# High-weight and low-weight products of a half of K issued in two runs of eight instead of in alternation

## The chip, the cores and the metric

The kernel runs on one core of one Trainium2 chip. The metric is the device time of one execution in microseconds (us); lower is better. Engine names in profile rows: PE is TensorE's products, PEld its weight loads, DVE is VectorE, ACT is ScalarE, POOL is GpSimd, SP is SyncE.

## The reference

A decoder trunk of two layers over 256 tokens of width 2048, in float32. Layer 0 has causal self-attention with 16 heads of 128, a T5 relative bias (with 256 tokens there is one block, so no gathered blocks); layer 1 has sliding-window attention (window 128) with 4 shared K/V heads and a sink for each head. Each layer then has a ConvFFN, and a LayerNorm follows each of the four parts:

```python
attn = moba_attention(h, ...) if layer < N_A_LAYERS else swa_attention(h, ...)
h = layer_norm(ALPHA * h + attn, ln_g[layer, 0], ln_b[layer, 0])
u = h @ w_up                               # 2048 -> 2 * 5504
hc = causal_depthwise_conv3(u) + conv_b
g, v = jnp.split(hc, 2, axis=-1)
h = layer_norm(ALPHA * h + (gelu(g) * v) @ w_down, ln_g[layer, 1], ln_b[layer, 1])
```

Nearly all of the arithmetic is `x @ W` with 256 rows of x and some 95 million weights, each of which is read once.

## The kernel before

**Precision.** Every float32 operand of a large product is split into a high part, its rounding to fp32r, and a low part, the rest. A product x @ W is made of three: high x with high W, low x with high W, high x with low W. `xT` holds x transposed, [128, 16 blocks of K, 512]: columns 0 to 255 are the high parts of the 256 tokens, columns 256 to 511 the low parts.

**Weights.** They arrive as one stream of halves, each [128, 1024] float32 (512 KB). SyncE loads a half into one of 4 `raw` buffers (L71), ScalarE copies it to the high part `wh` (L85), VectorE subtracts to get the low part `wl` (L86); there are 4 buffers of each. `take` hands out the next half, after it has issued the splits up to 3 halves ahead.

**Two kinds of unit.** Where the output is wanted transposed (Q and K in attention, the up-projection of the FFN) the weights are stationary: `ws_unit` makes 128 output features for 256 tokens from two halves, each eight blocks of K by 128 features. For each block j a 128x128 block of `wh` is loaded and 512 columns of `xT` stream through it (high and low x, into columns 0 to 511 of the accumulator `acc`, L224), and then the same block of `wl` is loaded and the 256 high columns stream (added to columns 0 to 255, L225). There are 222 such units, 444 halves: 32 units in attention of layer 0, 85 in each FFN and 20 in attention of layer 1. The first unit of each FFN goes another way (the `feed` branch, L203 to L219): all of its products have 256 columns, first alternating high and low weights (L208, L209), then sixteen with the high weights and the low x (L213). V and the output projections use activations as the stationary side (`Moving`): three products of 512 columns for each block (L244, L245, L246).

**Order.** The schedule is written out by hand: each engine runs its instructions in program order. `step` marks a slot at the end of each half; `at` puts work of ScalarE and VectorE into a later slot (it is issued by the next `take`, behind the splits), `pe_at` puts TensorE work of attention there. After a unit ScalarE copies columns 256 to 511 of `acc` (L532), VectorE adds columns 0 to 255 (L533), and in the FFN the convolution, gelu and gate follow (L534 to L543).

Of the kernel before, what the change touches and what calls it, by code (L numbers as in the profile page):

```python
# [46 lines left out]
def trunk(ctx: ExitStack, tc: tile.TileContext, wst, xT_in, x_in, relb, onehot, umask, sinks, conv_in, ln_g, ln_b, out):  # L47
# [26 lines left out]
    def split_upto(i):  # L74
        while todo["split"] <= min(i, n_halves - 1):
            s = todo["split"]
            r = raws.pop(s)
            if s in aside:
                j = aside.pop(s)
                wh, wl = (xT[:, k:k + 2, :].rearrange("p a b -> p (a b)") for k in (4 * j, 4 * j + 2))  # L80
            else:
                wh = spool.tile([P, HW], F32R, name="wh")
                wl = spool.tile([P, HW], F32R, name="wl")
            for c in pieces(s):
                nc.scalar.activation(wh[:, c], r[:, c], AF.Copy)  # L85
                nc.vector.tensor_tensor(out=wl[:, c], in0=r[:, c], in1=wh[:, c].bitcast(F32), op=ALU.subtract)  # L86
            halves[s] = (wh, wl)
            todo["split"] += 1
            load_weights()
# [13 lines left out]
    def run(agenda):  # L103
        for n in sorted(n for n in agenda if n <= slot["now"]):
            for f, a in agenda.pop(n):
                f(*a)

    def step():
        run(behind)
        slot["now"] += 1  # L110
# [3 lines left out]
    def take(ahead=AHEAD):  # L114
        i = nexth["i"]
        nexth["i"] += 1
        split_upto(i + ahead)
        run(before)
        return halves.pop(i)
# [75 lines left out]
    def ws_unit(acc, feed=None):  # L195

        def cols(w, j):
            return w[:, j * P:(j + 1) * P]  # L200

        o = acc[:, 0:T]
        if feed:  # L203
            pair = [take(1 - i) for i in range(2)]
            for k in range(KB):
                feed(k)
                wh, wl = pair[k // 8]
                nc.tensor.matmul(o, cols(wh, k % 8), xT[:, k, 0:T], start=(k == 0), stop=False)  # L208
                nc.tensor.matmul(o, cols(wl, k % 8), xT[:, k, 0:T], start=False, stop=False)  # L209
            feed(KB)  # L210
            split_upto(nexth["i"] + AHEAD - 2)
            for k in range(KB):
                nc.tensor.matmul(o, cols(pair[k // 8][0], k % 8), xT[:, k, T:2 * T], start=False, stop=(k == KB - 1))  # L213
                if k % 8 == 7:
                    step()
                    split_upto(nexth["i"] + AHEAD - 2 + (k + 1) // 8)
                    if k < 8:
                        run(before)
            return  # L219
        for hf in range(2):  # L220
            wh, wl = take()
            for j in range(8):
                k = hf * 8 + j
                nc.tensor.matmul(acc, cols(wh, j), xT[:, k, :], start=(k == 0), stop=False)  # L224
                nc.tensor.matmul(o, cols(wl, j), xT[:, k, 0:T], start=False, stop=(k == KB - 1))  # L225
            step()

# [208 lines left out]
    def layer_attention(l, rest):  # L436
        with tc.tile_pool(name=f"att{l}", bufs=2) as pool:
# [24 lines left out]
            def feat_unit(name, bufs):  # L462
                acc = acc_tile()
                ws_unit(acc)
                o = pool.tile([P, T], F32, name=name, bufs=bufs)

                def evac():
                    nc.scalar.activation(o, acc[:, T:2 * T], AF.Copy)
                    nc.vector.tensor_tensor(out=o, in0=acc[:, 0:T], in1=o, op=ALU.add)

                at(0, evac, first=True)
                return o
# [35 lines left out]
    def layer_ffn(l, rest):  # L508
        with tc.tile_pool(name=f"ffn{l}", bufs=2) as pool:
# [35 lines left out]
            for i in range(FT):  # L545
                g, v = (pool.tile([P, T], F32, name=f"c{s}") for s in range(2))
                for s, c in enumerate((g, v)):
                    first = i == 0 and s == 0
                    acc = acc_tile()
                    ws_unit(acc, feed if first else None)  # L550
                    at(0, conv, i, s, acc, first, c)
                    if s == 0:
                        at(1, nc.scalar.activation, c, c, AF.Gelu_apprx_tanh)
                at(0, gate, i, g, v)
                at(1, store, i, g)
# [93 lines left out]
```

## Time and profile before

| | |
|---|---|
| time, median of 3 runs | 2125.76 us (2123.73 to 2126.88) |
| profiled execution | 2124.89 us, span 2123.0 us |
| busy, share of the span | TensorE products 99%, weight loads 84%, VectorE 68%, ScalarE 47%, GpSimd 1% |
| HBM read | 401.02 MB, 192 GB/s over the span |

The span goes from the first to the last instruction. A weight load and the products around it overlap, and a product is recorded as busy for longer than the time until the next one starts; so two busy TensorE lines together exceed the span.

### The profile page before, as it was taken

To read this page: it belongs to the slowest core of one execution; us is meant where nothing else is said; L and a number is where in the kernel's file an instruction comes from. 1 tells how busy PE (TensorE), PEld (TensorE's weight loads), DVE (VectorE), ACT (ScalarE), POOL (GpSimd) and SP (SyncE) were. 2 spreads that over 40 slices of the span, in tenths; PEclk is the share of its full clock that TensorE was granted. 3 is DMA by queue.
4 is the path that set the end of the run, shared out by engine and by line. 5 is a ranking of instruction groups with operands and counts; after the bars stand their busy time and mean duration, and the time that the engine had idled before them with its cause. 6 is when DMAs were issued, how large, how long until landed. Compare 5 with 4: busy or idle time off the path is not lost.

```text
span 2123.0 us, 28513 instructions
## 1 busy us (share of the span) xinstructions
PE 2092.1 (99%) x10962; PEld 1785.8 (84%) x10962; DVE 1434.8 (68%) x2104; ACT 987.6 (47%) x1395; POOL 25.5 (1%) x40
## 2 busy tenths in 40 slices
PE   8999999999999999999999999999999999999997
PEld 6888888788888888888887888888888888888886
DVE  5555555787777787744456676687787787765455
ACT  5444444354445544433344554445544454443342
POOL 1100000000000000000001000000000000000000
PEclk9999999999999999999999999999999999999999
DMA  8855556565555555556666644565555555556663
GB/s 278 300 170 177 169 169 204 178 200 188 187 188 187 184 186 188 188 188 197 192 206 211 212 145 162 174 211 187 184 187 187 189 184 183 188 190 196 191 196 130
DMA packets 114120, 405.08 MB, mean 191 GB/s; under 512 B 15504, under 2 KB 15808, under 8 KB 112704
## 3 DMA queue, kind: packets, MB, share of 16 engines
q1 hardware_dynamic: 106848, 383.83, 55.6%
q0 software_dynamic: 7136, 19.44, 2.6%
q8 instruction: 86, 1.41, 0.3%
q14 instruction: 50, 0.41, 0.1%
HBM read 401.02 MB, written 6.34 MB: 192 GB/s over the span
## 4 chain that ended last, share of the span: by engine, by line
PE 97%; DVE 2%; ACT 0%; DMA 0%; issue 0%; SPq 0%; ACTq 0%; DVEq 0%
PE acc L224 39%; PE acc L225 20%; PE acc L245 11%; PE acc L246 11%; PE acc L244 11%; PE at L386 1%; PE at L419 1%; DVE wl L86 1%; PE at L412 0%; PE at L385 0%; DMA raw<-in_wst_dram 0%; PE at L420 0%; DVE xT L332 0%; DVE res L316 0%; DVE res L315 0%; PE at L325 0%
## 5 line engine op out<-in xcount | busy, mean ns | idle before, releaser
L86 DVE TENSOR_TENSOR wl<-raw,wh 128x1024 fp32r<-128x1024 f32 (+1 forms) x709 | 865.4, 1222 | 609.9 <-ACT wh L85 609.4
L224 PE MATMUL acc<-xT,wh 128*128 128x512 f32 x3552 | 1262.9, 401 | 0.0
L85 ACT ACTIVATE wh<-raw 128x1024 fp32r<-128x1024 f32 (+1 forms) x709 | 750.6, 1059 | 936.2 <-PE acc L246 331.7
L225 PE MATMUL acc<-xT,wl 128*128 128x256 f32 x3552 | 997.5, 281 | 0.0
L224 PEld LDWEIGHTS acc<-xT,wh 128*128 128x128 f32 x3552 | 667.8, 188 | 163.7
L225 PEld LDWEIGHTS acc<-xT,wl 128*128 128x128 f32 x3552 | 671.7, 189 | 0.9
L244 PE MATMUL acc<-wh,aT 128*128 128x512 f32 x656 | 255.7, 390 | 0.0
L246 PE MATMUL acc<-wh,aT 128*128 128x512 f32 x656 | 255.4, 389 | 0.0
L245 PE MATMUL acc<-wl,aT 128*128 128x512 f32 x656 | 255.4, 389 | 0.0
L246 PEld LDWEIGHTS acc<-wh,aT 128*128 128x128 f32 x656 | 123.1, 188 | 25.6
L244 PEld LDWEIGHTS acc<-wh,aT 128*128 128x128 f32 x656 | 123.2, 188 | 25.5
L245 PEld LDWEIGHTS acc<-wl,aT 128*128 128x128 f32 x656 | 123.2, 188 | 25.4
L244 PE MATMUL acc<-wh,oT 128*128 128x512 f32 x224 | 89.0, 398 | 0.0
L246 PE MATMUL acc<-wh,oT 128*128 128x512 f32 x224 | 87.4, 390 | 0.0
L245 PE MATMUL acc<-wl,oT 128*128 128x512 f32 x224 | 87.3, 390 | 0.0
L535 DVE SCALAR_TENSOR_TENSOR c<-h,cw,c 128x255 f32<-128x255 f32 x170 | 82.3, 484 | 6.0
L536 DVE SCALAR_TENSOR_TENSOR c<-h,cw,c 128x254 f32<-128x254 f32 x170 | 82.2, 484 | 6.1
L534 DVE TENSOR_SCALAR c<-h,cw 128x256 f32<-128x256 f32 x170 | 70.2, 413 | 6.1
L244 PE MATMUL acc<-wh,xT 128*128 128x512 f32 x160 | 65.9, 412 | 8.3 <-ACT wh L85 8.1
L533 DVE TENSOR_TENSOR h<-acc,h 128x256 f32<-128x256 f32 x170 | 71.0, 418 | 0.0
L542 ACT ACTIVATE aT<-c 128x256 fp32r<-128x256 f32 x86 | 36.0, 419 | 66.3 <-DVE c L539 66.3
L245 PE MATMUL acc<-wl,xT 128*128 128x512 f32 x160 | 64.1, 400 | 1.5 <-DVE wl L86 1.5
(102 smaller groups left out, 1193.3 us busy)
## 6 DMA issues: line engine op xcount, KB each, us to landing
raw<-in_wst_dram SPq DMA_DIRECT2D x723, 512.0 KB, 3.4
band<-ud POOLq DMA_DIRECT2D x8, 512.0 KB, 13.2
bias<-band POOLq DMA_DIRECT2D x8, 512.0 KB, 5.0
gb<-in_ln_g_dram POOLq DMA_DIRECT2D x4, 1024.0 KB, 5.8
gb<-in_ln_b_dram POOLq DMA_DIRECT2D x4, 1024.0 KB, 8.6
res<-in_x_dram POOLq DMA_DIRECT2D x2, 1024.0 KB, 9.6
out_dram<-res SPq DMA_DIRECT2D x8, 256.0 KB, 2.5
xc<-in_xT_dram SPq DMA_DIRECT2D x7, 256.0 KB, 7.3
```

The source lines that it names most:

```text
L85: nc.scalar.activation(wh[:, c], r[:, c], AF.Copy)
L86: nc.vector.tensor_tensor(out=wl[:, c], in0=r[:, c], in1=wh[:, c].bitcast(F32), op=ALU.subtract)
L224: nc.tensor.matmul(acc, cols(wh, j), xT[:, k, :], start=(k == 0), stop=False)
L225: nc.tensor.matmul(o, cols(wl, j), xT[:, k, 0:T], start=False, stop=(k == KB - 1))
L244: nc.tensor.matmul(acc, sh, wh, start=(k == 0), stop=False)
L245: nc.tensor.matmul(acc, sh, wl, start=False, stop=False)
L246: nc.tensor.matmul(acc, sl, wh, start=False, stop=(k == self.nk - 1))
L533: nc.vector.tensor_tensor(out=h, in0=acc[:, 0:T], in1=h, op=ALU.add)
L534: nc.vector.tensor_scalar(c, h, w[:, 2:3], w[:, 3:4], op0=ALU.mult, op1=ALU.add)
L535: nc.vector.scalar_tensor_tensor(c[:, 1:T], h[:, 0:T - 1], w[:, 1:2], c[:, 1:T], op0=ALU.mult, op1=ALU.add)
L536: nc.vector.scalar_tensor_tensor(c[:, 2:T], h[:, 0:T - 2], w[:, 0:1], c[:, 2:T], op0=ALU.mult, op1=ALU.add)
L542: nc.scalar.activation(aT[:, i, 0:T], g, AF.Copy)
```

## The change

In `ws_unit` the loop over the eight blocks of a half is split in two: first the eight products with `wh`, then the eight with `wl`. Operands, accumulator and the number of instructions are the same; `start` is still on the first product of the unit and `stop` on the last. The `feed` branch and `Moving` stay.

```diff
             for j in range(8):
                 k = hf * 8 + j
                 nc.tensor.matmul(acc, cols(wh, j), xT[:, k, :], start=(k == 0), stop=False)
+            for j in range(8):
+                k = hf * 8 + j
                 nc.tensor.matmul(o, cols(wl, j), xT[:, k, 0:T], start=False, stop=(k == KB - 1))
             step()
```

## Rows read from the trace of the kernel before

**Rows 1.** The page, parts 1 (busy us, share, instructions) and 4 (chain, shares).
```profile
PE 2092.1 (99%) x10962; PEld 1785.8 (84%) x10962; DVE 1434.8 (68%) x2104; ACT 987.6 (47%) x1395; POOL 25.5 (1%) x40
...
PE 97%; DVE 2%; ACT 0%; DMA 0%; issue 0%; SPq 0%; ACTq 0%; DVEq 0%
PE acc L224 39%; PE acc L225 20%; PE acc L245 11%; PE acc L246 11%; PE acc L244 11%; PE at L386 1%; PE at L419 1%; DVE wl L86 1%; PE at L412 0%; PE at L385 0%; DMA raw<-in_wst_dram 0%; PE at L420 0%; DVE xT L332 0%; DVE res L316 0%; DVE res L315 0%; PE at L325 0%
```

**Rows 2.** The page, costliest groups: count | busy us, mean ns | idle before.
```profile
L224 PE MATMUL acc<-xT,wh 128*128 128x512 f32 x3552 | 1262.9, 401 | 0.0
...
L225 PE MATMUL acc<-xT,wl 128*128 128x256 f32 x3552 | 997.5, 281 | 0.0
L224 PEld LDWEIGHTS acc<-xT,wh 128*128 128x128 f32 x3552 | 667.8, 188 | 163.7
L225 PEld LDWEIGHTS acc<-xT,wl 128*128 128x128 f32 x3552 | 671.7, 189 | 0.9
```

**Rows 3.** Line L224 in two stretches: count, durations, first and last start (us).
```profile
L224 PE MATMUL acc<-xT,wh x1303: 394/398/404, 419.6 to 879.7; 128*128 128x512 f32 x187
...
L224 PE MATMUL acc<-xT,wh x1331: 394/398/404, 1399.8 to 1869.7; 128*128 128x512 f32 x191
```

**Rows 4.** Timeline of TensorE, FFN of layer 0: start us, duration us, instruction.
```profile
816.06 0.40 PE L224 MATMUL acc<-xT,wh 128*128 128x512 f32 x1
816.29 0.28 PE L225 MATMUL acc<-xT,wl 128*128 128x256 f32 x1
816.41 0.40 PE L224 MATMUL acc<-xT,wh 128*128 128x512 f32 x1
816.65 0.28 PE L225 MATMUL acc<-xT,wl 128*128 128x256 f32 x1
816.77 0.40 PE L224 MATMUL acc<-xT,wh 128*128 128x512 f32 x1
817.01 0.28 PE L225 MATMUL acc<-xT,wl 128*128 128x256 f32 x1
817.12 0.40 PE L224 MATMUL acc<-xT,wh 128*128 128x512 f32 x1
```

**Rows 5.** Timeline of TensorE, attention of layer 0: first and ninth L224.
```profile
63.12 0.39 PE L224 MATMUL acc<-xT,wh 128*128 128x512 f32 x1
...
65.89 0.39 PE L224 MATMUL acc<-xT,wh 128*128 128x512 f32 x1
```

**Rows 6.** Timeline, down-projection of layer 0: first and fifteenth L244.
```profile
1000.07 0.39 PE L244 MATMUL acc<-wh,aT 128*128 128x512 f32 x1
...
1009.59 0.39 PE L244 MATMUL acc<-wh,aT 128*128 128x512 f32 x1
```

**Rows 7.** First unit of layer 1's FFN: loads of L213, and the timeline.
```profile
L213 PEld LDWEIGHTS acc<-xT,wh x16: 192/192/193, 1394.2 to 1396.0; 128*128 128x128 f32 x16
...
1394.32 2.08 PE L213 MATMUL acc<-xT,wh 128*128 128x256 f32 x16
1396.24 0.40 PE L224 MATMUL acc<-xT,wh 128*128 128x512 f32 x1
1396.47 0.28 PE L225 MATMUL acc<-xT,wl 128*128 128x256 f32 x1
```

**Rows 8.** Timeline: first and ninth of two streams of 512-column products.
```profile
888.49 0.40 PE L244 MATMUL acc<-wh,aT 128*128 128x512 f32 x1
...
890.36 0.40 PE L246 MATMUL acc<-wh,aT 128*128 128x512 f32 x1
...
86.25 0.39 PE L245 MATMUL acc<-wl,xT 128*128 128x512 f32 x1
...
88.10 0.39 PE L244 MATMUL acc<-wh,xT 128*128 128x512 f32 x1
```

**Rows 9.** Busy by stretch (granted clock, DMA, GB/s last); waits, 420 to 880 us.
```profile
408.00:888.00 480.00, 480.00 (x2719) 416.36 (x2718) 379.33 (x595) 238.05 (x340) 0.00 (x0) 1.00 0.59 191
...
ACT wh L85 <- PE acc L224: 63.3, 77, 1.1
```

## The prediction

> **What bounds the kernel now.** I read the page first. TensorE is busy for 2092.1 of 2123.0 us, and the chain that ended last is 97% TensorE: 39% lies on the high-weight product L224, 20% on the low-weight product L225 [rows 1]. So a gain or loss shows in the time only if it changes how fast one product follows the other on TensorE. A busy share of 99% does not say that the engine is at its best: the products overlap, so the number to read is the distance from one start to the next, not the duration. The list of costly groups gives durations of 401 and 281 ns for products that stream 512 and 256 columns, each with a weight load of its own of 188 or 189 ns, 3552 of each kind [rows 2].
>
> Next I took the distance between starts. In the up-projection of both FFNs, where nothing but these pairs runs on TensorE, 1303 starts of L224 span 419.6 to 879.7 us: 460.1 / 1302 = 0.3534 us a pair; the second layer gives 469.9 / 1330 = 0.3533 us [rows 3]. Half a unit (eight pairs) takes 8 x 0.3534 = 2.827 us. The timeline shows how a pair divides: the 512-column product holds the engine for 0.23, 0.24, 0.24 us in turn, the 256-column one for 0.12, 0.12, 0.11 us, and the pattern comes back after three pairs (816.06 to 817.12 us = 1.06 us) [rows 4].
>
> Then I looked for what either product costs among its own kind. A settled stream of 512-column products (the down-projection) runs 14 triples from 1000.07 to 1009.59 us: 9.52 / 42 = 0.2267 us each [rows 6]. Sixteen 256-column products in a row, L213, which read the same xT with a new weight block each, take 1394.32 to 1396.24 us: 1.92 / 16 = 0.120 us each, although their loads are recorded at 192 ns, so the loads overlap what goes before [rows 7]. The two add up to 0.3467 us, 6.7 ns below the pair of today. Alternating need not cost that much more: in one half in attention eight pairs run from 63.12 to 65.89 us, 0.346 us each [rows 5]. So TensorE has two ways through the same instructions, and the FFNs are in the slower one. That is not the clock: the granted clock is 1.00 over the FFN up-projection [rows 9].
>
> **What the change does, part by part.** It removes nothing and adds nothing: the same 7104 products with the same loads, in another order. Per half there are now eight 512-column products, then eight 256-column ones, so sixteen changes of width become two.
>
> *The eight low-weight products.* 8 x 0.120 = 0.960 us by L213 [rows 7]. The last of them is followed by a 512-column product; the alternation shows 0.11 to 0.12 us there [rows 4], so this end is right within 0.01 us.
>
> *The eight high-weight products.* If they ran settled from the first one on: 8 x 0.2267 = 1.813 us. But the trace shows that a 512-column stream does not settle at once. Behind the pairs of the FFN, the first eight of the down-projection run from 888.49 to 890.36 us: 1.87 us, 0.057 above settled. Behind the small products of attention (after the first one, which also waits them out), eight run from 86.25 to 88.10 us: 1.85 us, 0.037 above [rows 8]. Eight products in a row are thus mostly inside this settling. Which entry fits? No row has a run of 512s behind a run of 256s; the nearest is the one L224 behind the sixteen L213, and it held the engine for 0.23 us (1396.24 to 1396.47 us) [rows 7], not 0.24 as the first one at 888.49 us. So I take 1.85 us and keep 1.813 and 1.87 us as ends.
>
> *Half a unit after:* 1.85 + 0.96 = 2.81 us against 2.827: a gain of 0.017 us. Ends: 1.813 + 0.96 = 2.773 (gain 0.054) and 1.87 + 0.96 = 2.83 (loss 0.003).
>
> *How often.* 85 units x 2 halves x 2 FFN layers = 340 halves; at 0.017 us: 5.8 us. The other 52 units (104 halves) lie in attention, where some halves run at 0.346 us a pair already [rows 5] and would lose 2.81 - 2.77 = 0.04 us, and others run as the FFN's do. I take one in four as fast (a choice): 104 x (0.75 x 0.017 - 0.25 x 0.04) = 0.3 us. Together 6.1 us.
>
> *Waits.* No wait is added. The wait for the low weights moves from the second product of a half to the ninth, which only relaxes it. The high-weight buffer is read for the last time by the eighth product instead of the fifteenth: from 7 x 0.353 = 2.47 us into the half to 7 x 0.23 = 1.6 us, about 0.9 us earlier. ScalarE waits for just that in 77 cases between 420 and 880 us, 63.3 us in total [rows 9], so its next copy (L85) starts earlier, with the evacuation of the previous unit queued behind it. I cost this at nothing: ScalarE is busy 238.05 of 480 us and VectorE 379.33 of 480 there, while TensorE is busy for all 480 [rows 9], so copies already lead the products. The low-weight buffer is still freed by the last product of the half and the raw buffer after VectorE's split, so the loads start no earlier and collide with nothing new; 191 GB/s becomes some 1% more at most [rows 9]. If that cover were gone, the cost would show as TensorE idle before L224 or L225, and both stand at 0.0 us now [rows 2].
>
> [...] The rows give the product N/2.4 GHz plus 13 ns, for 512 columns (213 + 13) and for 256 (107 + 13) [rows 6, 7]. [...]
>
> **Sum.** Profiled execution before: 2124.89 us, with 2123.0 us of span and 1.9 us around it; the median of the runs is 2125.76, 0.9 us more, which I leave as scatter. 2124.9 - 6.1 = 2118.8 us.
>
> **Rivals.**
> 1. *Runs settle at once.* The slow way needs the alternation, and an eight runs at 0.2267 us each. For it: settled streams and L213 hold their pace over a whole run [rows 6, 7]. Against: the two settlings of rows 8. Time: 340 x 0.054 = 18.4 us, plus at most 78 x 0.054 = 4.2 us in attention: 2124.9 - 22.6 = 2102.3 us.
> 2. *The settling eats it all, or order is neutral.* At 1.87 us a run, the entry seen behind the FFN's pairs [rows 8], halves lose 0.003 us: +1 us, and the fast halves of attention (26 x 0.06) another 1.6 us: 2127.5 us; strictly neutral: 2124.9. For it: 1.87 is the entry behind the very same weights and data layout. Against: the first product behind L213 takes 0.23, not 0.24 us [rows 7]. [...]
> 3. *Slower: every high-weight product keeps its slow gap.* Place: L224. Today's 0.23, 0.24, 0.24 us (mean 0.2367) would belong to a 512-column product in this stage, and the 0.11 to 0.12 of the 256s, which give part of it back, would become a flat 0.120. Then a half takes 8 x (0.2367 + 0.120) = 2.853 us, +0.026: 340 x 0.026 = 8.8 us, and in attention up to 104 x 0.026 = 2.7: 2136.4 us. It decides once eight 512s take over 2.827 - 0.96 = 1.867 us, 0.2334 each. For it: L224 is recorded with 0.40 us in the FFN against 0.39 for the settled stream [rows 4, 6], and the first one behind L213 is already slow [rows 7]. Against: fast pairs exist with the same operands [rows 5], and the settling of rows 8 falls with every product.
>
> **How the numbers follow.** Chances: partial settling, my forecast, 45% (own range 2111 to 2121 us, an entry cost of 0.015 to 0.045 us a half); rival 1, 15%; rival 2, 25%; rival 3, 15%. The predicted time is the first: 2118.8 us. The range reaches down to rival 1, 2103, and up past rival 2 into the lower part of rival 3, 2130 us; outside stay most of rival 3 and the last of rival 1, together under 2 in 10. A change of under 0.2% (4.25 us) can't be told from none here. Faster than that: nearly all of the first case (its top edge lies at the bound, 2120.6) and rival 1: 57%. Within 0.2%: rival 2 and that edge: 27%. Slower: rival 3 and a tail of rival 2: 16%.
>
> **What would show it.** In the profile after, starts of the high-weight products in an FFN: my forecast wants the eight of a half to take about 1.85 us, with gaps near 0.235 first and near 0.228 last, and the eight low-weight ones 0.96. Gaps of 0.227 from the first on are rival 1; 1.87 us is rival 2; a steady 0.237 is rival 3. TensorE's idle before the two lines should stay near 0, and the down-projections, the norms and the granted clock as they are. I am wrong if the eight low-weight products don't hold 0.120 us behind 512-column ones, of which no row speaks, or if a wait for weights appears before TensorE.

## The result and the profile after

The median is 2110.04 us (4 runs, 2109.25 to 2110.67) against 2124.82 us before (4 runs beside them): a ratio of 0.9929, 95% interval 0.9912 to 0.9946. The kernel became 0.7% faster: 14.8 us where 6.1 were forecast. The time lies inside the range (2103 to 2130), in the first case's direction and just below its own range (2111 to 2121).

The page after, parts 1 and 4, and of part 5 the lines that answer to [rows 2] (L224 is still the high-weight product, L227 is now the low-weight one; the lines behind it moved down by two):

```profile
PE 2077.3 (99%) x10962; PEld 1788.2 (85%) x10962; DVE 1434.7 (68%) x2104; ACT 989.1 (47%) x1395; POOL 25.5 (1%) x40
...
PE 97%; DVE 2%; ACT 0%; issue 0%; DMA 0%; SPq 0%; ACTq 0%; DVEq 0%
...
L224 PE MATMUL acc<-xT,wh 128*128 128x512 f32 x3552 | 896.3, 394 | 0.0
L224 PEld LDWEIGHTS acc<-xT,wh 128*128 128x128 f32 x3552 | 640.8, 189 | 116.0
L227 PEld LDWEIGHTS acc<-xT,wl 128*128 128x128 f32 x3552 | 484.5, 190 | 34.8
L227 PE MATMUL acc<-xT,wl 128*128 128x256 f32 x3552 | 495.2, 282 | 0.0
```

The same 10962 products, still 97% of the chain, and no idle time of TensorE before either line; the mean high-weight product is recorded with 394 ns instead of 401. Do not read a gain out of the busy column: 1262.9 became 896.3 us only because neighbours of one line now overlap and are counted once. The distance between starts is again the number to read. Timeline of TensorE after, in the FFN of layer 0; the second and third lines come from narrow windows (from 421.93 and from 422.16 us) and show the fifth and the sixth of the eight products:

```profile
420.82 2.00 PE L224 MATMUL acc<-xT,wh 128*128 128x512 f32 x8
421.75 0.39 PE L224 MATMUL acc<-xT,wh 128*128 128x512 f32 x1
421.98 0.39 PE L224 MATMUL acc<-xT,wh 128*128 128x512 f32 x1
422.66 1.12 PE L227 MATMUL acc<-xT,wl 128*128 128x256 f32 x8
423.61 0.63 PE L224 MATMUL acc<-xT,wh 128*128 128x512 f32 x2
```

Eight high-weight products take 422.66 - 420.82 = 1.84 us: the first four 0.93 us (0.2325 each), the last four 0.91 (0.2275), so the settling of [rows 8] is there. It is over after five products: the last three take 422.66 - 421.98 = 0.68 us, the settled 0.227 each. The low-weight eight take 0.95 us (0.119 each). Half a unit is 2.79 us against 2.827 [rows 3].

Where the 14.7 us of the profiled executions (2124.89 to 2110.16 us) lie is read from the first pair of an FFN and the first product of its down-projection (L246, before L244):

```profile
406.85 0.40 PE L224 MATMUL acc<-xT,wh 128*128 128x512 f32 x1
...
881.72 0.40 PE L246 MATMUL acc<-wh,aT 128*128 128x512 f32 x1
...
1387.28 0.40 PE L224 MATMUL acc<-xT,wh 128*128 128x512 f32 x1
...
1862.15 0.40 PE L246 MATMUL acc<-wh,aT 128*128 128x512 f32 x1
```

Before, the second and third of these points stood at 888.49 us [rows 8] and 1396.24 us [rows 7], the first and the last here:

```profile
407.96 0.40 PE L224 MATMUL acc<-xT,wh 128*128 128x512 f32 x1
...
1876.77 0.40 PE L244 MATMUL acc<-wh,aT 128*128 128x512 f32 x1
```

Each FFN's pairs went from 480.53 to 474.87 us: 11.3 us in the two, 5.66 / 170 = 0.033 us a half. Up to the first FFN 1.1 us were gained, and 2.2 us from the first down-projection to the second FFN (507.75 to 505.56). Neither is all order. Four stretches show it, before and then after: attention of layer 0 (from its first unit to the long output projection), from there to the pairs of the FFN, and the same two in layer 1 (columns: length, PE, PEld, DVE, ACT, POOL busy, granted clock, DMA share, GB/s):

```profile
32.58:318.94 286.36, 286.36 (x1550) 246.30 (x1548) 159.46 (x252) 135.58 (x229) 8.63 (x11) 1.00 0.61 201
318.94:407.96 89.02, 84.58 (x407) 71.25 (x406) 60.94 (x73) 38.04 (x44) 2.72 (x4) 0.98 0.53 178
1153.38:1305.89 152.51, 152.51 (x877) 133.62 (x876) 104.20 (x224) 81.36 (x179) 1.86 (x3) 1.00 0.54 183
1305.89:1396.24 90.35, 85.98 (x408) 72.63 (x406) 60.92 (x73) 38.03 (x44) 1.59 (x3) 0.96 0.55 182
```
```profile
32.83:317.18 284.35, 284.35 (x1549) 246.80 (x1548) 159.51 (x252) 136.29 (x229) 8.64 (x11) 1.00 0.62 203
317.18:406.85 89.67, 85.70 (x407) 72.20 (x406) 60.92 (x73) 38.05 (x44) 2.71 (x4) 0.96 0.55 180
1146.43:1298.31 151.88, 151.88 (x878) 133.90 (x876) 104.11 (x224) 83.00 (x179) 1.86 (x3) 1.00 0.55 179
1298.31:1387.28 88.97, 84.55 (x407) 71.22 (x406) 60.92 (x73) 38.04 (x44) 1.60 (x3) 0.98 0.55 179
```

Attention gained 2.0 and 0.6 us at a granted clock of 1.00. The stretches ahead of the FFNs, where norm and transposes let TensorE wait, go with the granted clock instead (1.00 is 2.4 GHz; below it, part of the stretch ran at the other level, 1.2 GHz): 89.0 us at 0.98 and 89.7 to 90.4 us at 0.96, in both kernels. Ahead of the first FFN the kernel after had the lower clock and lost 0.65 us; ahead of the second the kernel before had it, and 1.4 us were gained there.

### The profile page after: what moved, and what is told of

The parts are those of the page before. It is cut to its first block, busy times and chain, and to the rows that moved or that the text cites. A ratio compares the mean times of both kernels' runs of the same rounds, so it can differ in the third digit from the quotient of the medians.

```text
span 2108.3 us, 28513 instructions
## 1 busy us (share of the span) xinstructions
PE 2077.3 (99%) x10962; PEld 1788.2 (85%) x10962; DVE 1434.7 (68%) x2104; ACT 989.1 (47%) x1395; POOL 25.5 (1%) x40
## 4 chain that ended last, share of the span: by engine, by line
PE 97%; DVE 2%; ACT 0%; issue 0%; DMA 0%; SPq 0%; ACTq 0%; DVEq 0%
PE acc L224 39%; PE acc L227 20%; PE acc L247 12%; PE acc L246 12%; PE acc L248 12%; PE at L388 1%; PE at L421 1%; DVE wl L86 1%; PE at L414 0%; DVE res L317 0%; PE at L387 0%; PE at L422 0%; DVE res L318 0%; DVE xT L334 0%; PE at L327 0%
## 5 line engine op out<-in xcount | busy, mean ns | idle before, releaser
L224 PE MATMUL acc<-xT,wh 128*128 128x512 f32 x3552 | 896.3, 394 | 0.0
L224 PEld LDWEIGHTS acc<-xT,wh 128*128 128x128 f32 x3552 | 640.8, 189 | 116.0
L227 PEld LDWEIGHTS acc<-xT,wl 128*128 128x128 f32 x3552 | 484.5, 190 | 34.8
L227 PE MATMUL acc<-xT,wl 128*128 128x256 f32 x3552 | 495.2, 282 | 0.0
L246 PE MATMUL acc<-wh,aT 128*128 128x512 f32 x656 | 255.5, 389 | 0.0
L246 PEld LDWEIGHTS acc<-wh,aT 128*128 128x128 f32 x656 | 123.2, 188 | 25.6
L246 PE MATMUL acc<-wh,oT 128*128 128x512 f32 x224 | 88.9, 397 | 0.0
L246 PE MATMUL acc<-wh,xT 128*128 128x512 f32 x160 | 65.7, 411 | 8.7 <-ACT wh L85 8.5
```

The source lines that it names most:

```text
L246: nc.tensor.matmul(acc, sh, wh, start=(k == 0), stop=False)
```

## The experiments

In all of them the FFN's up-projection is read, where only the two products run on TensorE. Of the settled paces, 0.2267 and 0.120 us, a half would be 2.773 us. The granted clock is 1.00 there in every run. The diffs are against the kernel before unless said otherwise; they are shortened, `...` stands for what is left out, and their comments are added here.

**Mirrored halves.** Is it the width or the start of a half that costs? In the change both fall together. Here the second half starts with the low weights.

```diff
+            for f in ((low, high) if hf else (high, low)):   # eight products each
+                f()
```

> The change, but in the second half of a unit the low weights come first, then the high ones: runs of 16 low products in each unit and of 16 high ones across units. Theory (a 512-column product behind 256-column ones settles over some five products, for 0.028 us): one settling a unit in place of two, so a unit of 2 x 2.794 = 5.588 us falls to about 16 x 0.2267 + 0.028 + 16 x 0.120 - 0.007 = 5.568 us; 170 FFN units save 3.3 us, attention, where other products break the runs, some 0.5: about 2106 us, and the ninth high product in a row stands at 0.227 us. Rival (the slow gaps belong to the start of a half, where TensorE takes up new buffers, and not to the width): each half's first high products stay at 0.233 to 0.236 us, 2110 us.

Measured: 2109.01 us (5 runs), ratio 0.9922 (0.9910 to 0.9935). Timeline:

```profile
502.96 2.08 PE L229 MATMUL acc<-xT,wl 128*128 128x256 f32 x16
504.87 3.82 PE L225 MATMUL acc<-xT,wh 128*128 128x512 f32 x16
508.53 2.08 PE L229 MATMUL acc<-xT,wl 128*128 128x256 f32 x16
510.44 1.78 PE L225 MATMUL acc<-xT,wh 128*128 128x512 f32 x7
```

Sixteen high-weight products, across the start of a half, take 508.53 - 504.87 = 3.66 us: 1.84 + 8 x 0.2267 = 3.65. The second eight are settled, and a unit takes 5.57 us, as expected. So the slow gaps belong to the change of width and not to the start of a half. The total moved less than the FFNs' 3.3 us: the two stretches of attention took 285.07 and 152.25 us, 1.1 us more than after the change (284.35 and 151.88), and the interval overlaps the change's.

**Runs of four and of two.** The same loops with shorter runs:

```diff
+            for j0 in range(0, 8, 4):                        # or 2
+                for j in range(j0, j0 + 4): ...              # high weights
+                for j in range(j0, j0 + 4): ...              # low weights
```

> Runs of four high and four low products instead of eight. Theory (settling by position in the run): twice 0.233 + 0.236 + 0.228 + 0.233 and 0.117 + 3 x 0.120 = 2.814 us a half, +0.020 on the change: about 2118.5 us. Rival (a fixed price for each change of width, 0.021 us there and back): 2.773 + 0.042 = 2.815 us, the same; only runs of two tell these apart.

> Runs of two. Theory (settling by position): four times 0.233 + 0.236 + 0.117 + 0.120 = 2.824 us a half, close to the alternation's 2.827: about 2123 us. Rival (fixed price of 0.021 us for each change there and back): 2.773 + 4 x 0.021 = 2.857 us: about 2137 us, slower than before.

Measured: 2115.52 us for four (0.9953, 0.9940 to 0.9967) and 2108.16 us for two (0.9922, 0.9907 to 0.9938). Timelines, first of four, then of two:

```profile
510.00 1.09 PE L225 MATMUL acc<-xT,wh 128*128 128x512 f32 x4
510.93 0.64 PE L228 MATMUL acc<-xT,wl 128*128 128x256 f32 x4
511.41 1.09 PE L225 MATMUL acc<-xT,wh 128*128 128x512 f32 x4
...
515.62 0.63 PE L225 MATMUL acc<-xT,wh 128*128 128x512 f32 x2
```
```profile
500.00 0.62 PE L225 MATMUL acc<-xT,wh 128*128 128x512 f32 x2
500.46 0.40 PE L228 MATMUL acc<-xT,wl 128*128 128x256 f32 x2
500.70 0.63 PE L225 MATMUL acc<-xT,wh 128*128 128x512 f32 x2
...
515.33 0.62 PE L225 MATMUL acc<-xT,wh 128*128 128x512 f32 x2
```

Runs of four: 510.00 to 515.62 us are four groups, 2.81 us a half. Runs of two: 500.00 to 515.33 us are 22 groups or 44 pairs, 0.3484 us a pair, 2.787 us a half. The rival, a fixed price for each change of width, wanted 2.857 and 2137 us: it is out. But my own theory, a high-weight product's gap by its position in the run, wanted 2.824 us and falls too. Runs of two are no worse than runs of eight, with four times as many changes. In runs of two a group takes 15.33 / 22 = 0.697 us. Its two high-weight products cost 0.46 to 0.47 us, 0.01 to 0.02 above settled; so the two low-weight ones take some 0.23, below their settled 0.24, and give part of it back. What counts is the sequence, not the number of changes.

**Other widths, alternating.** The low-weight product streams more columns; the kernels do more work than the reference asks, so only their pace is of use.

```diff
-                nc.tensor.matmul(o, cols(wl, j), xT[:, k, 0:T], ...)
+                nc.tensor.matmul(acc[:, 0:384], cols(wl, j), xT[:, k, 0:384], ...)   # or 448, 512
```

> The order of before, alternating, but the low-weight product streams 384 columns in place of 256 (it adds low x times low weights for half of the tokens: more work, not less). Theory A (a 256-column product ends just as the next weight load does, at 0.120 us, and that is what unsettles the next 512-column product): with 384 columns the load has 0.053 us to spare, both kinds are settled, 0.227 + 0.173 = 0.400 us a pair: about 2290 us. Theory B (any change of width unsettles it, by the same 7 ns a pair): 0.407 us a pair: about 2315 us.

> The order of before, alternating, 448 columns in each low-weight product (more work, as above). Settled would be 0.2267 + 0.200 = 0.4267 us a pair. Theory 1 (the excess of a pair does not shrink with the difference in width: 0.0067 us at 256 columns, 0.0133 at 384): 0.433 to 0.440 us. Theory 2 (448 is nearly 512, and 512 had none): under 0.430 us. Times about 2124.8 + 3552 x (pair - 0.3533): 2408 to 2433 us, or under 2397 us.

> The order of before, alternating high and low weights, but the low-weight product streams all 512 columns (adds low x times low weights: more work). Theory (unequal widths are what costs): with equal widths no excess, 0.4533 us a pair: 2124.8 + 3552 x 0.100 = 2480 us. Rival (changing between the high and the low weight buffers costs, whatever the width): 0.460 us a pair or more: 2504 us.

Measured: 2336.89, 2424.08 and 2482.96 us, one execution each. Line L224 in a stretch of the FFN (count, durations, first and last start), for 384, 448 and 512 columns:

```profile
L224 PE MATMUL acc<-xT,wh x1312: 396/398/402, 438.1 to 979.9; 128*128 128x512 f32 x188
```
```profile
L224 PE MATMUL acc<-xT,wh x1143: 394/397/398, 499.8 to 999.8; 128*128 128x512 f32 x191
```
```profile
L224 PE MATMUL acc<-xT,wh x1104: 389/389/389, 499.9 to 1000.0; 128*128 128x512 f32 x184
```

The pairs take 541.8 / 1311 = 0.4133, 500.0 / 1142 = 0.4378 and 500.1 / 1103 = 0.4534 us; settled they would take 0.400, 0.4267 and 0.4533 (for 384 and 448 columns an estimate, 0.1733 and 0.200 us for the low-weight product, on the straight line through 0.120 and 0.2267 us at 256 and 512). So the excess is 13 ns at 384, 11 at 448, none at 512, and 6.7 at 256 (before). With equal widths, alternating between the weight buffers costs nothing. With 384 the next weight load has more time than with 256, yet the excess doubles: my theory A, that the load is only just covered by the short product, is out, and even a product shorter by an eighth pays.

**Another bank.** In the FFN the low-weight products go to an accumulator of their own (left out of the output).

```diff
+                lo = psum.tile([P, 512], F32, name="at")     # once a unit
+                nc.tensor.matmul(lo[:, 0:T], cols(wl, j), xT[:, k, 0:T], start=(k == 0), stop=(k == KB - 1))
```

> The order of before; in the FFN units the low-weight products go to an accumulator of their own in another bank, which is not read (the output lacks high x times low weights there). Theory P (the slow pairs come from products of two widths adding into the same columns of one bank): 0.3467 us a pair, 471 us for an FFN's pairs, about 2106 us. Theory W (the width of the stream alone counts): 0.3533 us, 480.5 us, 2125 us.

Measured: 2127.13 us, one execution. Timeline:

```profile
499.84 0.40 PE L224 MATMUL acc<-xT,wh 128*128 128x512 f32 x1
500.07 0.28 PE L228 MATMUL at<-xT,wl 128*128 128x256 f32 x1
...
501.96 0.40 PE L224 MATMUL acc<-xT,wh 128*128 128x512 f32 x1
```

Six pairs take 2.12 us, 0.3533 each, to the digit what they took in one bank. That both products add into one bank has no part in it.

**The change with 384 columns.** Does grouping give back the larger excess too? Against the kernel of the change:

```diff
-                nc.tensor.matmul(o, cols(wl, j), xT[:, k, 0:T], ...)
+                nc.tensor.matmul(acc[:, 0:384], cols(wl, j), xT[:, k, 0:384], ...)
```

> The change, with 384 columns in each low-weight product (adds low x times low weights for half of the tokens: more work). Alternating with 384 columns took 0.4133 us a pair, 0.0133 above the settled 0.2267 + 0.1733. Theory (a change of width costs, its own kind does not): eight high ones about 0.03 us above settled, the low ones settled: 1.84 + 1.387 = 3.23 us a half, an FFN's pairs 549 us instead of 562, about 2300 us. Rival (the 384-column product itself is dear, 0.176 us, and the high one with it): 8 x 0.4133 = 3.307 us a half, 2337 us.

Measured: 2321.24 us, one execution, 15.7 us under the alternation with 384.

```profile
501.98 2.01 PE L224 MATMUL acc<-xT,wh 128*128 128x512 f32 x8
503.83 1.58 PE L227 MATMUL acc<-xT,wl 128*128 128x384 f32 x8
505.25 2.01 PE L224 MATMUL acc<-xT,wh 128*128 128x512 f32 x8
```

A half takes 3.27 us, between theory (3.23) and rival (3.307): the high-weight eight 1.85 as expected, but the 384-column eight 1.42 instead of 1.387. The high-weight gaps do not settle in the order seen in the change (the sixth is 0.236 us in this trace, 0.227 there), so five products are no rule. The 384-column ones pay for the change of width too, which the 256-column ones do not: those only gain behind 512.

**Alternation, entered differently.** One fast half in attention [rows 5] left open whether the FFN could be brought into the fast way. The low product runs one block behind.

```diff
+                if j:
+                    low(j - 1)
+            low(7)
```

> Alternation with the low product one block behind: H0 H1 L0 H2 L1 ... H7 L6 L7 in each half, so each half has two equal neighbours at either end. Theory (the pace of an alternation depends on the phase in which it is entered, and a pair of equal neighbours moves the phase): the pairs between may fall into the fast way, 0.347 us each, 2.78 us a half, about 2106 us. Rival (alternation as such costs 0.3533 us a pair in the FFN however it is entered): six or seven slow pairs a half, 2.82 us: about 2121 us.

Measured: 2121.30 us (0.9982, 0.9972 to 0.9991). Timeline; the line numbers are those of this kernel, where L228 is the high weight:

```profile
500.68 0.40 PE L224 MATMUL acc<-xT,wl 128*128 128x256 f32 x2
500.92 0.63 PE L228 MATMUL acc<-xT,wh 128*128 128x512 f32 x2
501.38 0.28 PE L224 MATMUL acc<-xT,wl 128*128 128x256 f32 x1
...
503.50 0.40 PE L224 MATMUL acc<-xT,wl 128*128 128x256 f32 x2
```

A half takes 2.82 us, as the rival had it. Two equal neighbours at either end don't move the alternation into its fast way.

**The best of both.** Mirrored halves in the FFN, runs of two in attention.

> The FFN with the mirrored order (high, low | low, high), attention with runs of two. By the stages of the two kernels that it joins: 170 FFN units at 473.19 us a layer and attention at 372.96 and 240.68 us give about 2105 us, 1 to 3 us under the runs of two (2108.2) and 4 under the mirrored order (2109.0). Rival (a stage's pace depends on the state in which the stage before leaves TensorE): FFN or attention keep another pace than there, and the time lies at 2109 us or above.

Measured: 2107.79 us (4 runs, 0.9918, 0.9904 to 0.9933); the rival's 2109 is missed, the expected 2105 too. The FFN keeps its pace: in its trace the pairs run from 406.42 to 879.62 us, 473.2 us as in the mirrored kernel. Behind that FFN attention of layer 1 keeps the time that it has in the kernel with runs of two, 151.71 us; the stretch from there to the second FFN does not (runs of two first, then this kernel):

```profile
406.42 1.78 PE L224 MATMUL acc<-xT,wh 128*128 128x512 f32 x7
...
879.62 0.39 PE L253 MATMUL acc<-wh,aT 128*128 128x512 f32 x1
```
```profile
1144.40:1296.11 151.71, 151.71 (x878) 133.20 (x876) 104.23 (x224) 81.41 (x179) 1.86 (x3) 1.00 0.55 182
1296.11:1385.08 88.97, 84.54 (x408) 71.20 (x407) 60.94 (x73) 38.05 (x44) 1.59 (x3) 0.98 0.53 180
```
```profile
1144.96:1296.67 151.71, 151.71 (x878) 133.19 (x876) 104.23 (x224) 81.41 (x179) 1.87 (x3) 1.00 0.54 182
1296.67:1386.08 89.41, 85.44 (x407) 71.95 (x406) 60.93 (x73) 38.04 (x44) 1.60 (x3) 0.96 0.54 180
```

So the rival is out: the stages taken over from the two kernels keep their times. Most of what is missing to the expected time lies, against the kernel with runs of two, with the norms at lower granted clocks: 0.44 us ahead of the second FFN (0.96 against 0.98), 0.85 ahead of the first (0.96 against 0.98) and 0.6 between the first FFN and attention of layer 1 (0.99 against 1.00).

Mirrored, runs of two and this one lie within 1.3 us of each other. Their medians are 1.0 to 2.3 us below the change's, each measured beside the kernel before and not beside the change, and the intervals overlap: all are faster than the kernel before, but faster than the change is shown only by the FFN's rows (473.2 against 474.87 us).

## Why the prediction was right, and what it mis-sized

*The bound.* Right: TensorE's spacing sets the end, the clock in the FFN is 1.00 before and after, and what a half gains there arrives in the time: 340 x 0.033 = 11.3 us.

*The eight low-weight products.* 0.96 us forecast, 0.95 measured: the eight keep the 0.120 of [rows 7] but for the start: behind the settled high-weight run the second product follows the first after 0.113 us, the mean of the 170 halves of the first FFN.

*The eight high-weight products.* 1.85 us taken, 1.84 measured. The choice of the milder entry, by the one L224 behind L213 in [rows 7], was right; the settling in fact is over after five products.

*The mis-sized term.* The gain of a half, 0.017 us, was a difference of 2.81 and 2.827 us. Each of the two parts was some 0.01 us too long, about 1% of it or less, and the difference came out as half of the measured 0.033. The range carried this; the single value could not, from rows that are read to 0.01 us.

*How often.* The FFN's count was right. The other stages were given 0.3 us and gave about 3.4: 2.6 in attention and 0.7 as the balance of the two stretches ahead of the FFNs, where the granted clock did not stay as it was, though the prediction had wanted it to. Attention's share of fast halves was a guess and too high: in the trace of before 8 of its 104 halves take 2.77 us, not 26. That this balance added to the gain and did not take from it is luck.

*Waits.* None appeared. ScalarE's waits for the high-weight product are what they were (420 to 880 us after; 63.3 us in 77 before [rows 9]):

```profile
ACT wh L85 <- PE acc L224: 59.6, 78, 1.3
```

*The rivals.* Runs do not settle at once (first four gaps 0.2325), the settling does not eat it all, and no product keeps its slow gap. That the order is neutral is contradicted by the 0.7%. Where neighbours have equal widths, the gap of N columns here is N/2.4 GHz plus 13 ns (0.2267 us for 512, with alternating weights too, and 0.120 for 256), each product with a weight load of its own. The Trainium skill ("TensorE: Matmul & The Clock Gate", "Back-to-back issue gap") gives N/2.4 + 2.5 ns as the gap of an isolated product at the full clock, and says that in a stream of weight loads and products both set the spacing. The trace agrees that the isolated gap is not reached in such a stream; no run here leaves the loads out, so what the other 11 ns are is not shown.

*What stays open.* Shown is that neighbours of unequal width cost in the FFN, in an amount that depends on the sequence, and that the bank, the weight buffer and the start of a half are not the cause; that the short product leaves too little time for the load is contradicted. Why TensorE needs several products to come back to its pace, and why some halves in attention alternate at the fast one, no run shows.

## What to carry to other kernels

Where TensorE is busy to 99%, read the distance between starts and compare it with what each product takes among its own kind: 0.3534 us a pair against 0.2267 + 0.120 showed what there was to gain, 0.054 us a half, of which the change took 0.033; no wait or busy share showed it. Products of unequal width that depend on nothing between them are worth grouping or at least pairing, by measurement: runs of 1, 2, 4, 8 and 16 gave 2.827, 2.787, 2.81, 2.79 and 2.785 us a half, so neither longer nor fewer is a rule. A forecast that is a small difference of two long times should be given as a range first.

## What the runs showed of the hardware

- A product's spacing depends on its neighbours: a 512-column product follows another after 0.2267 us, but takes 0.2325 us on average in the first four behind 256-column ones.
- The cost is not monotonic in the width: alternating 512 with 256, 384, 448 and 512 columns costs 6.7, 13, 11 and 0 ns a pair above settled (settled is an estimate at 384 and 448).
- It is indifferent to the accumulator's bank (0.3533 us a pair in one or in two) and to alternating weight buffers (0.4534 us at equal widths).
- With the clock granted in full, stages keep their times to 0.01 us when another stage is reordered: attention of layer 1 took 151.71 us in both kernels with runs of two there, behind FFNs of two paces (473.7 and 473.2 us).
